# Seven products over all sixteen blocks, sums on GpSimd and four weight buffers in a decoder block's input projection

## The chip, the core and the metric

The kernel runs on one core of a Trainium2 chip. The metric is the device time of one launch in microseconds (us); the time before is 2086.86 us, the median of three runs (2086.74 to 2087.18). PE is TensorE's matmul queue and PEld its weight loads, DVE is VectorE, ACT is ScalarE, POOL is GpSimd, SP the engine that issues most transfers.

## The reference, cut to what matters

The program is one decoder block over 512 positions of width 2048 in float32: an RMSNorm, one input projection whose columns are shared out among two attention mixers (8 heads of dilated attention, 8 heads of compressed, selected and window attention), an output projection, a SwiGLU FFN of width 5632, and a final RMSNorm. What the change touches is the input projection of the normed input:

```
h = rmsnorm(x, norm1_g)        # 512 x 2048
z = h @ w_in                   # the columns are q, k, v of both mixers
```

A column block of `w_in` (128 columns) is a tensor called qb, qa, ka, va, ks, kw, vs or vw in the kernel. 2048 rows are 16 blocks of 128. The norm's per-position factor is applied behind the product (tile `r`), the gain `norm1_g` ahead of it.

## The kernel before, in words

Every float32 product is made from three matmuls (function `mm`, lines 302 to 304): both operands are split into a high part (a rounded copy, written by ACT) and a low part (source minus high, written by DVE); high times high, high times low and low times high are added up in PSUM. Weights arrive by DMA as units of 128x1024 float32 in five tiles called `raw` and are split into tiles called `w`; the unit of that work is a half, at most 128x512, called a `Job`: `first` (line 176) has ACT write the high part, `second` (line 190) has DVE write the low part and then runs `post`, which may form sums in `raw` for later halves or load the next unit. `next_half` hands PE the halves in order; when PE's code comes to half i, the code of ACT's high part for half i+3 and of DVE's low part for half i+2 has been put out. Every engine runs its own instructions strictly in that order.

Two column blocks (qb with qa, ka with va, and so on) form a pair, and a pair is computed by a scheme with seven products in place of eight (Strassen and Winograd), over two column blocks, two halves of the positions (`LO`, `HI`, 256 each) and two halves of the 2048 rows. Here a half of the rows has M = 7 blocks, so 14 of the 16 blocks are in the scheme: products P1 to P7, each 7 blocks times 3 matmuls of 256 positions. The two blocks left over are computed directly: X for the first column block, Y for the second, each 2 blocks times 3 matmuls of 512 positions. The first operands (tiles `ah`/`al` for the plain ones, T2, T3 and T4 for sums) are made once, during the first column blocks (`mix_parts`); the weights' sums are made for each pair:

- P1's operand is a unit as loaded; a transfer on POOL's queue with an accumulating write (line 137) forms the first operand of P5.
- Behind P5's second half DVE adds two units into P6's operand (line 236), and POOL issues an accumulating transfer that makes P7's operand (line 242).
- Behind P2's halves POOL issues accumulating transfers from tile to tile (line 248) that make P3's operand; for ks/vs DVE does it.

There are 17 pairs, called pair 0 to pair 16 here: ka/va of head 0, then qb/qa and ka/va of heads 1 to 7, with ks/kw and vs/vw ahead of head 4. The order within a pair is the tuple `PAIR` (line 221). Behind each half `side_hook` puts out one step of the attention of the head before (scores `psc`, transposes `pt`, products `po`, all on PE; soft maximum on DVE and ACT). `AFTER_T` is a table of halves whose split weights are placed 32 words in (`MH`) and not 16 (`WH`). Five `w` tiles take turns. Pair 0 runs while the first operands' sums for blocks 4 to 6 are still being made. After the pairs come the output projection (`pab`) and the FFN, which is 1446 us of the time.

## Time and profile before

| what | value |
|---|---|
| time, median of 3 runs | 2086.86 us |
| time of the profiled execution | 2088.05 us |
| its span (first to last instruction) | 2086.3 us |
| PE / PEld busy | 2070.6 us (99%) / 1993.7 us (96%) |
| DVE busy | 1752.7 us (84%) |
| ACT busy | 1355.5 us (65%) |
| POOL busy | 389.3 us (19%) |
| granted TensorE clock | 0.998 |
| the 17 pairs with the attention between them | 147.0 to 608.6 us |

A row of the timeline gives the start in us from the span's start, the duration in us, the engine, the line, the operation, the tiles (output<-inputs), the form and the count; in brackets stands idle time of the engine just ahead and who ended it. Matmuls are pipelined, so a matmul's own duration is longer than what it costs: the cost is the distance from one start to the next. A group row gives count, busy us, mean ns of one, idle us ahead and who ended it.

### The profile page before, as it was taken

The page shows a single profiled execution, that of the slowest core. Times are in us where ns is not written, and L with a number is a line of the kernel's source. Part 1 is how long each engine was busy: PE and PEld are TensorE (multiplying, and loading weights), DVE is VectorE, ACT ScalarE, POOL GpSimd, SP SyncE. Part 2 cuts the span into 40 slices and gives each one's busy share as a digit, 9 for nine tenths or more (in the row PEclk, how much of TensorE's full clock was granted, in tenths as well). Part 3 has the DMA queues.
Part 4 walks back from the last instruction along what each step waited for, and adds up shares of the span by engine and source line. Part 5 has one row for each costly group of instructions (what it writes and reads, how often), then busy time and mean ns, then how long its engine had stood idle before and what let it go on. Part 6 is the DMA issues. An engine that isn't in the chain of part 4 may idle for free.

```text
span 2086.3 us, 44180 instructions
## 1 busy us (share of the span) xinstructions
PE 2070.6 (99%) x16297; PEld 1993.7 (96%) x16297; DVE 1752.7 (84%) x3831; ACT 1355.5 (65%) x3355; POOL 389.3 (19%) x487
## 2 busy tenths in 40 slices
PE   9999999999999999999999999999999999999998
PEld 8789999999988889999999999999999999999997
DVE  6778888788887589989989898988889898888885
ACT  6566666566664356585767667685857676676856
POOL 0011111111120002021322213130303122030323
PEclk9999999999999999999999999999999999999999
DMA  7466665666564235366776869694847567494982
GB/s 243 156 208 163 164 154 135 168 155 146 146 217 161 97 106 175 109 215 161 185 190 168 211 146 225 152 213 118 210 130 189 147 169 175 133 211 123 217 245 94
DMA packets 138298, 351.02 MB, mean 168 GB/s; under 512 B 15328, under 2 KB 39392, under 8 KB 138080
## 3 DMA queue, kind: packets, MB, share of 16 engines
q1 hardware_dynamic: 76384, 235.44, 33.8%
q0 software_dynamic: 61552, 112.69, 29.1%
q8 instruction: 128, 2.10, 0.4%
q14 instruction: 90, 0.74, 0.1%
q10 hardware_dynamic: 144, 0.07, 0.0%
HBM read 268.89 MB, written 72.35 MB: 164 GB/s over the span
## 4 chain that ended last, share of the span: by engine, by line
PE 95%; DVE 2%; DMA 2%; ACT 1%; issue 0%; POOL 0%; SPq 0%; DVEq 0%; POOLq 0%; ACTq 0%
PE P L302 18%; PE P L304 18%; PE P L303 18%; PE pp L304 5%; PE pp L302 5%; PE pp L303 5%; PE pab L298 3%; PE pab L299 3%; PE pab L297 3%; PE pd L302 1%; PE pd L303 1%; PE pd L304 1%; PE pt L969 1%; PE pp L299 1%; PE pp L298 1%; PE pp L297 1%
## 5 line engine op out<-in xcount | busy, mean ns | idle before, releaser
L176 ACT ACTIVATE w<-raw 128x512 fp32r<-128x512 f32 (+2 forms) x1058 | 598.7, 594 | 300.5 <-DVE raw L1348 121.3
L190 DVE TENSOR_TENSOR w<-raw,w 128x512 fp32r<-128x512 f32 (+2 forms) x1024 | 659.3, 658 | 112.0 <-ACT w L176 109.7
L302 PE MATMUL P<-ah,w 128*128 128x256 f32 x1616 | 447.1, 277 | 0.0
L304 PE MATMUL P<-ah,w 128*128 128x256 f32 x1616 | 447.1, 277 | 0.0
L303 PE MATMUL P<-al,w 128*128 128x256 f32 x1616 | 446.8, 276 | 0.0
L304 PEld LDWEIGHTS P<-ah,w 128*128 128x128 f32 x1616 | 303.5, 188 | 0.3 <-DVE w L190 0.2
L302 PEld LDWEIGHTS P<-ah,w 128*128 128x128 f32 x1616 | 303.6, 188 | 0.1
L303 PEld LDWEIGHTS P<-al,w 128*128 128x128 f32 x1616 | 303.5, 188 | 0.0
L1697 POOL DMA_DIRECT2D sums<-stg x240 | 198.3, 874 | 429.1 <-ACT P L1690 150.8
L214 DVE TENSOR_TENSOR w<-raw,w 128x256 fp32r<-128x256 f32 x480 | 186.7, 420 | 28.2 <-ACT w L210 26.1
L1348 DVE TENSOR_TENSOR raw<-raw 128x512 f32<-128x512 f32 x274 | 188.5, 688 | 3.4
L210 ACT ACTIVATE w<-raw 128x256 fp32r<-128x256 f32 x480 | 177.0, 410 | 4.8 <-DVE raw L1426 4.8
L302 PE MATMUL pp<-ah,w 128*128 128x256 f32 (+1 forms) x544 | 164.1, 302 | 0.5 <-DVE pp L726 0.5
L304 PE MATMUL pp<-ah,w 128*128 128x256 f32 (+1 forms) x544 | 160.3, 295 | 1.5 <-DVE w L190 1.1
L303 PE MATMUL pp<-al,w 128*128 128x256 f32 (+1 forms) x544 | 159.2, 293 | 0.0
L1690 ACT ACTIVATE stg<-P 128x256 f32<-128x256 f32 x280 | 105.5, 381 | 15.3 <-DMA sums<-stg 5.8
L304 PEld LDWEIGHTS pp<-ah,w 128*128 128x128 f32 x544 | 102.3, 188 | 6.0 <-DVE w L190 2.9
L1352 POOL DMA_DIRECT2D raw<-in_wst_dram x40 | 34.3, 859 | 379.5 <-ACT w L176 174.9
L302 PEld LDWEIGHTS pp<-ah,w 128*128 128x128 f32 x544 | 102.7, 189 | 2.6 <-issue 0.6
L303 PEld LDWEIGHTS pp<-al,w 128*128 128x128 f32 x544 | 102.6, 189 | 1.9
L302 PE MATMUL pp<-T,w 128*128 128x256 f32 x357 | 101.7, 285 | 0.0
L297 PE MATMUL pab<-ah,w 128*128 128x512 f32 x256 | 100.6, 393 | 0.0
(399 smaller groups left out, 6161.7 us busy)
## 6 DMA issues: line engine op xcount, KB each, us to landing
raw<-in_wst_dram SPq DMA_DIRECT2D x390, 512.0 KB, 4.3
sums<-stg POOLq DMA_DIRECT2D x160, 256.0 KB, 7.0
raw<-in_wst_dram POOLq DMA_DIRECT2D x34, 448.0 KB, 6.6
raw<-in_wst_dram POOLq DMA_DIRECT2D x40, 256.0 KB, 4.7
sums<-stg POOLq DMA_DIRECT2D x80, 128.0 KB, 6.5
xc<-in_xt_dram SPq DMA_DIRECT2D x16, 256.0 KB, 3.5
bias<-in_bias_dram SPq DMA_DIRECT2D x16, 256.0 KB, 3.6
hs<-in_xt_dram SPq DMA_DIRECT2D x16, 256.0 KB, 5.2
```

The source lines that it names most:

```text
L176: act.activation(h, src, AF.Copy, scale=sign)
L190: dve.tensor_tensor(l, src, h.bitcast(F32), op=OP.subtract)
L210: act.activation(h, src(), AF.Copy)
L214: dve.tensor_tensor(l, src(), h.bitcast(F32), op=OP.subtract)
L297: pe.matmul(o, wh, mh, start=start, stop=False)
L298: pe.matmul(o, wh, ml, start=False, stop=False)
L302: pe.matmul(o, wh, mh, start=start, stop=False, skip_group_check=True)
L303: pe.matmul(o, wh, ml, start=False, stop=False, skip_group_check=True)
L304: pe.matmul(o, wl, mh, start=False, stop=stop, skip_group_check=True)
L1348: return lambda: dve.tensor_tensor(o(), o(), x(), op=OP.add)
L1690: return lambda: act.activation(o, a, AF.Copy)
L1697: return lambda s=sums[x]: pool_e.dma_start(kept_sums[k][:, q:q + n, :], s, **how)
```

## The change

M becomes 8: each of the seven products runs over 8 blocks, in two halves of 4, and X and Y are gone. A pair has 14 halves of 128x512 in place of 16 of 512, 384 or 2 times 128. P2's second half stands behind P6 now: P1 P1 P5 P5 P2 P6 P6 P2 P7 P7 P3 P3 P4 P4. The weights' sums behind P5 and P2 are made by GpSimd instructions on the tiles, not by DVE and by accumulating transfers; P7's operand is the difference of P6's and P4's. The three sums of the first operands are made by GpSimd for blocks above 4, with another sign for T2, and the order of these blocks is 4, 7, 5, 6. The eighth block's T2 and T3 lie in the fifth `w` tile (`w4`, called `tx`) and its T4 in free places of the attention's tile `et`; from the first pair to the output projection four `w` tiles take turns. The table `AFTER_T` is a new one for the new numbering (60 entries).

```diff
-M = 7
-MC = 128 * M
+M = 8
+KEPT = 7
...
+    w_used = {f"w{n}": n - 5 for n in range(5)}
+
     def wsplit(even):
-        return both(wp, 512, MH if even else WH, tag=turn("w", 5), name="w")
+        i = state["split"]
+        tag = min((t for t in w_used if t != "w4" or not n_few <= i < n_out), key=w_used.get)
+        w_used[tag] = i
+        return both(wp, 512, MH if even else WH, tag=tag, name="w")
...
-    PAIR = ("P1", "P5", "P2", "P6", "X", "P7", "P3", "Y", "P4")
+    PAIR = (("P1", 0), ("P1", 1), ("P5", 0), ("P5", 1), ("P2", 0), ("P6", 0), ("P6", 1), ("P2", 1), ("P7", 0), ("P7", 1),
+            ("P3", 0), ("P3", 1), ("P4", 0), ("P4", 1))
...
         def add(n, m, c):
-            dve.tensor_tensor(raws[u + n][:, c], raws[u + n][:, c], raws[u + m][:, c], op=OP.add)
+            pool_e.tensor_tensor(raws[u + n][:, c], raws[u + n][:, c], raws[u + m][:, c], op=OP.add)
 
         def after_p5(c):
-            if c.stop == MC:
+            add(0, 1, c)
+            if c.start:
                 for k in COLS:
-                    add(0, 1, k)
-                pool_e.dma_start(raws[u + 1][:, :MC], wst[u][:, :MC], accum_op=OP.add)
+                    pool_e.tensor_tensor(raws[u + 1][:, k], raws[u][:, k], raws[u + 3][:, k], op=OP.subtract)
 
         def after_p2(c):
-            if units[u][1] in ("ks", "vs"):
-                add(2, 0, c)
-            else:
-                pool_e.dma_start(raws[u + 2][:, c], raws[u][:, c], accum_op=OP.add)
+            add(2, 0, c)
+            if c.start:
+                load_to(u + 6)
...
         def sums():
-            dve.tensor_tensor(y[:, HI], y[:, HI], x[:, HI], op=OP.subtract)
-            dve.scalar_tensor_tensor(x[:, HI], y[:, HI], -1.0, x[:, LO], op0=OP.mult, op1=OP.subtract)
-            dve.scalar_tensor_tensor(x[:, LO], x[:, HI], -1.0, y[:, LO], op0=OP.mult, op1=OP.subtract)
+            if i > 4:
+                pool_e.tensor_tensor(y[1], y[1], x[:, HI], op=OP.subtract)
+                pool_e.tensor_tensor(x[:, HI], y[1], x[:, LO], op=OP.add)
+                pool_e.tensor_tensor(x[:, LO], x[:, HI], y[0], op=OP.subtract)
+                return
...
-        for name in PAIR:
-            if name in "XY":
-                h, l = next_half()
-                now_in[0] = 0
-                p = a if name == "X" else b
-                for k in range(2):
-                    c = slice(128 * k, 128 * k + 128)
-                    mm(p, h[:, c], l[:, c], ah[:, 2 * M + k, :], al[:, 2 * M + k, :], False, False)
...
+        for name, part in PAIR:
+            p, c = place_of[name]
+            h, l = next_half()
+            now_in[0] = 1
+            for n in range(4):
+                k = 4 * part + n
+                w = slice(128 * n, 128 * n + 128)
+                mm(p[:, c], h[:, w], l[:, w], *mix_at(operand[name], k), name == "P1" and k == 0,
+                   name in ("P3", "P4") and k == M - 1)
```

Three places show how instructions move. The first is PE in pair 0, behind P6. Before, X stands there (the first three of its six rows; tile `pp` is the pair's PSUM bank, `psc` an attention step):

```order
L299 MATMUL psc<-kall,qb 128x288
L953 MATMUL psc<-sm,tmp 128x32 [waits DMAHW3_49]
L302 MATMUL pp<-ah,w 128x512 [waits Activation_49]
L303 MATMUL pp<-al,w 128x512
L304 MATMUL pp<-ah,w 128x512 [waits DVE_49]
```

In the changed kernel P2's second half stands there, in twelve matmuls of 256 in place of X's six of 512 (the first three are shown):

```order
L285 MATMUL psc<-kall,qb 128x288
L969 MATMUL psc<-sm,tmp 128x32 [waits DMAHW3_49]
L288 MATMUL pp<-ah,w 128x256 [waits Activation_49]
L289 MATMUL pp<-al,w 128x256
L290 MATMUL pp<-ah,w 128x256 [waits DVE_49]
```

What moved is X's work, into the products; the attention's steps around it stay.

The second place is POOL's queue over one pair in the middle. Before it holds only the issues of transfers:

```order
L242 DMA raw<-in_wst_dram 128x896 [waits DMASW5_49,DMASW6_49,DMASW1_49,DMAHW0_49,DVE_49,Activation_49]
L137 DMA raw<-in_wst_dram 128x896 [waits DMAHW5_49,DMAHW3_49,DMASW2_49]
L248 DMA raw<-raw 128x512 [waits DMASW4_49,DMAHW1_49,DMASW3_49,DVE_49]
L248 DMA raw<-raw 128x384 [waits DVE_49]
L1158 DMA o_69<-oh 128x512 [waits Activation_49]
```

In the changed kernel it holds six sums, in the order P6's two halves, P7's two, P3's two:

```order
L226 TENSOR_TENSOR raw<-raw 128x512 [waits DMAHW3_49,DMASW2_49,DVE_49]
L226 TENSOR_TENSOR raw<-raw 128x512 [waits DVE_49]
L232 TENSOR_TENSOR raw<-raw 128x512 [waits DMAHW5_49,Pool_49]
L232 TENSOR_TENSOR raw<-raw 128x512 [waits Pool_49]
L137 DMA raw<-in_wst_dram 128x1024 [waits DMAHW6_49]
L226 TENSOR_TENSOR raw<-raw 128x512 [waits DMAHW4_49,DVE_49]
L226 TENSOR_TENSOR raw<-raw 128x512 [waits DVE_49]
L1174 DMA o_77<-oh 128x512 [waits Activation_49]
```

Of four transfers one is left; six instructions came in, and three of them wait only for DVE or POOL itself.

The third place is ACT in pair 0, from the high part of P5's second half on. Before, T2, T3 and T4 of a block (`T_748` and so on) wait for DVE, and P7's weights wait for a transfer:

```order
L176 ACTIVATE w<-raw 128x384 [waits DVE_49]
L562 ACTIVATE T_748<-mx 128x256 [waits DVE_49]
L562 ACTIVATE T_749<-my 128x256
L562 ACTIVATE T_750<-mx 128x256 [waits DVE_49]
L176 ACTIVATE w<-raw 128x128 x2
L176 ACTIVATE w<-raw 128x512 [waits DMASW3_49,PE_49]
L905 ACT_TABLE_LOAD
```

In the changed kernel P6's two halves and the last block's T2 and T4 wait for POOL:

```order
L177 ACTIVATE w<-raw 128x512 [waits Pool_49]
L177 ACTIVATE w<-raw 128x512 [waits PE_49,Pool_49]
L571 ACTIVATE T_748<-mx 128x256 [waits Pool_49]
L571 ACTIVATE T_749<-my 128x256
L571 ACTIVATE T_750<-mx 128x256 [waits Pool_49]
L778 ACTIVATE slots<-pp 128x256 [waits PE_49,Activation_49]
L177 ACTIVATE w<-raw 128x512
L177 ACTIVATE w<-raw 128x512 [waits DVE_49,PE_49]
L921 ACT_TABLE_LOAD
```

What moved is the waited-for engine: a sum on GpSimd stands ahead of P6's weights and of the last block's operands, and no transfer stands ahead of P7's weights.

More of the change, by code (lines that the diff above doesn't have):

```diff
@@ L136, in load_to @@
             if units[u][0] == "pair" and units[u][4] == 0:
-                later(3 if pos["half"] else 0, lambda t=t, u=u: pool_e.dma_start(t[:, :MC], wst[u + 3][:, :MC], accum_op=OP.add))
+                later(3 if pos["half"] else 0, lambda t=t, u=u: pool_e.dma_start(t, wst[u + 3], accum_op=OP.add))
             if units[u] == ("quad", 0, 1):
@@ L253, in pair_jobs @@
         js = []
-        for name in PAIR:
-            if name in "XY":
-                n = 2 * int(name == "Y")
-                js.append(Job(lambda n=n: [(raws[u + n + i][:, MC:], 1.0 - n) for i in range(2)], even=True,
-                              pieces=True, post=more(7 if n else 5)))
-                continue
-            n = {"P1": 1, "P5": 0, "P6": 0, "P2": 2, "P7": 1, "P4": 3, "P3": 2}[name]
-            for c in COLS:
-                post = {"P5": lambda c=c: after_p5(c), "P2": lambda c=c: after_p2(c)}.get(name)
-                if c.stop == MC:
-                    post = {"P7": more(6), "P4": more(8)}.get(name, post)
-                js.append(Job(part(n, c), post=post, even=len(jobs) + len(js) in AFTER_T))
+        for name, k in PAIR:
+            n = {"P1": 1, "P5": 0, "P6": 0, "P2": 2, "P7": 1, "P4": 3, "P3": 2}[name]
+            c = COLS[k]
+            post = {"P5": lambda c=c: after_p5(c), "P2": lambda c=c: after_p2(c)}.get(name)
+            if k:
+                post = {"P7": more(6), "P3": more(7), "P4": more(8)}.get(name, post)
+            js.append(Job(part(n, c), post=post, even=len(jobs) + len(js) in AFTER_T))
         return js
     for u, d in enumerate(units):
+        if d == ("in", "qb", 0, 0):
+            n_few = -(-len(jobs) // 5) * 5
         if d[0] == "pair":
@@ L428, in block_kernel, with mix_at @@
         mixed[n] = tuple(a[:, b:b + M, c] for a in (ah, al))
+    def mix_at(n, i):
+        return (beyond if n in beyond and i == KEPT else {n: [t[:, i, :] for t in mixed[n]]})[n]
+    beyond = {}
     def tmp(n, name="tmp"):
@@ L511, in block_kernel @@
     hooks = [0]
-    mix_in = {}
+    mix_in, mix_y = {}, {}
     raw = []
@@ L519, in mix_load @@
                 t = area(n)
-                mixed[n] = tuple(t[:, at:at + M * 256].rearrange("p (k c) -> p k c", c=256) for at in (0, M * 256))
-        if i == 4:
+                mixed[n] = tuple(t[:, at:at + KEPT * 256].rearrange("p (k c) -> p k c", c=256)
+                                 for at in (0, KEPT * 256))
+                beyond[n] = None
+        if i == KEPT:
+            x = ap_.tile([128, S], F32, tag="slots", name="mx")
+            y = [late["pool"].tile([128, 384], F32, tag=t, name="my")[:, :256] if t else None for t in ("e2", None)]
+        elif i == 4:
             t = late["pool"].tile([128, 2 * S + 64], F32, tag="qa", name="mxy")
@@ L535, in mix_load_y @@
     def mix_load_y(i):
-        pool_e.dma_start(mix_in[i][1], xt[M + i])
+        y = mix_in[i][1]
+        if i < KEPT:
+            pool_e.dma_start(mix_y[i], xt[M + i])
+            return
+        y[1] = late["pool"].tile([128, 384], F32, tag="e1", name="my")[:, :256]
+        for c, t in zip((LO, HI), y):
+            pool_e.dma_start(t, xt[M + i][:, c])
     def raw_load():
@@ L591, in lows @@
             low("T2", x[:, HI])
-            low("T3", y[:, HI])
+            low("T3", y[1])
             low("T4", x[:, LO])
@@ L1236, in block_kernel @@
     late["pool"] = attn.enter_context(tc.tile_pool(name="attn2", bufs=1))
-    et_h, et_l = (t.rearrange("p (a b) -> p a b", b=128) for t in both(late["pool"], 13 * 128, MH, name="et"))
+    et = placed(late["pool"], 26 * 128, MH, name="et").rearrange("p (a b) -> p a b", b=128)
+    et_h, et_l = et[:, :13, :], et[:, 13:, :]
     late["e3"] = late["pool"].tile([128, 4, 3, 32], F32, name="ecs")
@@ L1289, in block_kernel @@
             raw_load()
-            for i in range(4, M):
+            for i in (4, 5, 7, 6):
                 mix_load(i)
-            for i in range(4, M):
-                mix_load_y(i)
+                if i < KEPT:
+                    mix_load_y(i)
             SCALE_X, SCALE_Y, DIFF, SUMS, HIGHS, LOWS = range(6)
```

103 lines of the change are left out of this document (49 added, 54 removed).

## The prediction

> **What bounds the kernel now.** I read the page's shares and chain first, then the stage table, then the distance from one matmul's start to the next.
>
> ```profile
> span 2086.3 us, 44180 instructions
> PE 2070.6 (99%) x16297; PEld 1993.7 (96%) x16297; DVE 1752.7 (84%) x3831; ACT 1355.5 (65%) x3355; POOL 389.3 (19%) x487
> PE 95%; DVE 2%; DMA 2%; ACT 1%; issue 0%; POOL 0%; SPq 0%; DVEq 0%; POOLq 0%; ACTq 0%
> ```
>
> PE is busy 99% of the span and is 95% of the chain that ended last. So time is won by giving PE less to stream, and lost where PE waits. The stages that the change touches (us, then busy us and count of PE, PEld, DVE, ACT, POOL): before the pairs, pair 0, a qb/qa pair, a ka/va pair, the stretch behind the pairs.
>
> ```profile
> 110.00:147.00 37.00, 36.98 (x196) 31.18 (x194) 26.32 (x54) 24.73 (x54) 6.22 (x11) 1.00 0.72 228
> 147.00:173.20 26.20, 24.89 (x187) 23.40 (x186) 23.63 (x75) 18.41 (x54) 3.41 (x4) 1.00 0.67 173
> 229.10:258.20 29.10, 28.95 (x222) 27.80 (x221) 24.05 (x66) 17.94 (x46) 5.15 (x6) 1.00 0.60 149
> 469.30:497.60 28.30, 28.30 (x220) 27.36 (x219) 24.29 (x79) 19.41 (x58) 4.93 (x6) 1.00 0.61 152
> 608.60:640.00 31.40, 30.20 (x154) 24.79 (x153) 20.82 (x48) 17.87 (x39) 1.60 (x3) 1.00 0.42 142
> ```
>
> PE is idle for 1.31 us in pair 0 (26.20 - 24.89), 0.15 and 0.00 us in the two later pairs, and 1.20 us behind the pairs. DVE has 4 to 5 us to spare in a pair, POOL over 20. Almost nothing but PE's own stream is left to win in the pairs.
>
> **The stream.** All of the 17 pairs' matmuls of 512 positions and, as one of two groups, those of 256:
>
> ```profile
> L302 PE MATMUL pp<-ah,w 128*128 128x512 f32 x68 | 28.3, 416 | 0.0
> L302 PE MATMUL pp<-ah,w 128*128 128x256 f32 x476 | 135.8, 285 | 0.5 <-DVE pp L726 0.5
> ```
>
> X and Y are 68 x 3 = 204 matmuls of 512; they go. Seven products get one more block, 7 x 3 = 21 matmuls of 256 in each pair, 357 in all. What one costs is the distance of starts, and the trace has two levels. At the fast one, X of one pair (six matmuls, first start to the next half's start) and a run of 51 matmuls of 256:
>
> ```profile
> 273.24 0.39 PE L302 MATMUL pp<-ah,w 128*128 128x512 f32 x1
> ...
> 274.60 0.28 PE L302 MATMUL pp<-T,w 128*128 128x256 f32 x1
> ```
>
> ```profile
> 398.02 0.28 PE L302 MATMUL pp<-ah,w 128*128 128x256 f32 x1
> ...
> 403.80 0.40 PE L302 MATMUL pp<-ah,w 128*128 128x512 f32 x1
> ```
>
> That is 1.36/6 = 0.2267 us and 5.78/51 = 0.1133 us: a matmul of 512 costs exactly two of 256, so splitting it up costs nothing by itself. At the slow level, which follows transposes until a half with the other placement has passed, five of 512 and nine of 256:
>
> ```profile
> 243.87 0.39 PE L303 MATMUL pp<-al,w 128*128 128x512 f32 x1
> ...
> 245.03 0.40 PE L297 MATMUL psc<-ka,qa 128*128 128x512 f32 x1
> ```
>
> ```profile
> 266.80 0.28 PE L302 MATMUL pp<-ah,w 128*128 128x256 f32 x1
> ...
> 267.86 0.29 PE L297 MATMUL psc<-kall,qb 128*128 128x288 f32 x1
> ```
>
> 1.16/5 = 0.232 us and 1.06/9 = 0.1178 us. All fast: 204 x 0.2267 = 46.2 us go, 357 x 0.1133 = 40.4 come, -5.8. All slow: 47.3 against 42.1, -5.3. I take **-5.5**; the ends are old ones fast and new ones slow, -4.1, and the reverse, -6.9.
>
> The new placement table moves the levels of the 2499 matmuls that stay (147 x 17). X and Y always had the other placement and so ended slow stretches; without them the new order has, by my count of halves behind transposes, about five in a hundred more at the slow level: 2499 x 0.05 x 0.0045 = 0.6 us. I take **+0.4**, bounds -0.6 to +0.8.
>
> **DVE's and ACT's work.** The groups of the splits and of the sums that go:
>
> ```profile
> L190 DVE TENSOR_TENSOR w<-raw,w 128x512 fp32r<-128x512 f32 x119 | 81.5, 685 | 14.4 <-ACT w L176 14.4
> L190 DVE TENSOR_TENSOR w<-raw,w 128x384 fp32r<-128x384 f32 x118 | 65.2, 553 | 4.2 <-ACT w L176 3.6
> L190 DVE TENSOR_TENSOR w<-raw,w 128x128 fp32r<-128x128 f32 x34 | 8.3, 287 | 0.5 <-ACT w L176 0.5
> L188 DVE SCALAR_TENSOR_TENSOR w<-raw,w 128x128 fp32r<-128x128 f32 x34 | 8.3, 285 | 0.0
> L236 DVE TENSOR_TENSOR raw<-raw 128x512 f32<-128x512 f32 x19 | 13.0, 687 | 0.1
> ```
>
> For each pair DVE loses four small splits (1.14 us) and two sums (0.69 and about 0.55), and seven splits grow from 384 to 512 (7 x 0.132 = 0.92): -1.46 us.
>
> **GpSimd's sums** come in, six of 128x512 a pair. The trace has only sums of 128x256, at the end of the kernel:
>
> ```profile
> L1964 POOL TENSOR_TENSOR sacc<-sacc,sqt x24: 732/758/1112, 2033.8 to 2070.6; 128x256 f32<-128x256 f32 x24
> 2061.25 0.88 POOL L1964 TENSOR_TENSOR sacc<-sacc,sqt 128x256 f32<-128x256 f32 x1 [0.38 <-ACT sqt L1962]
> 2062.51 0.77 POOL L1964 TENSOR_TENSOR sacc<-sacc,sqt 128x256 f32<-128x256 f32 x1 [0.39 <-ACT sqt L1962]
> 2061.77 0.90 DVE L1952 TENSOR_TENSOR hs<-hs,r 128x512 f32<-128x512 f32 x1
> 2063.05 0.78 DVE L1952 TENSOR_TENSOR hs<-hs,r 128x512 f32<-128x512 f32 x1
> 2064.41 0.68 DVE L1952 TENSOR_TENSOR hs<-hs,r 128x512 f32<-128x512 f32 x1
> ```
>
> One of 512 lies between one of 256 (0.74 us) and twice the slowest ordinary one (1.76 us); I take 1.5, since work doubles and a fixed part doesn't: 9 us of POOL a pair, which has room. The last three rows show a price: DVE's sum of two SBUF tiles takes 0.68 us alone, 0.90 and 0.78 us where a GpSimd sum runs into it. So a GpSimd sum of 256 takes 0.10 to 0.22 us from DVE, one of 512 perhaps double, 0.2 to 0.44: 1.2 to 2.6 us a pair if each meets such work. Against -1.46 that is -0.3 to +1.1 us on 24.3 busy of 28.3: DVE stays short of PE. [...]
>
> The sums' lateness: P5's first low part is written about when PE starts the half two ahead, then the sum, then ACT's high part of P6, wanted three halves (4 us of matmuls) ahead of P6. There is about 1 us to spare, and the transfers that ACT waited for (the 3.19 us below) go. **The four `w` tiles** let ACT start a half only when PE has left the one four before; by the starts of ACT's rows most high parts come later than that anyway, and the others stand well ahead of PE. Both edits at **+0.5** for the 16 later pairs: bounds -0.8 (all idle there is) and +4 (0.25 us a pair).
>
> **Pair 0.** The stalls:
>
> ```profile
> 150.07 0.36 PE L302 MATMUL pp<-ah,w 128*128 128x256 f32 x1 [0.46 <-DVE pp L726]
> 153.71 0.39 PE L304 MATMUL pp<-ah,w 128*128 128x256 f32 x1 [0.69 <-DVE w L190]
> 165.16 0.38 PE L304 MATMUL pp<-ah,w 128*128 128x256 f32 x1 [0.16 <-DVE w L190]
> 159.57 0.63 ACT L176 ACTIVATE w<-raw 128x512 fp32r<-128x512 f32 x1 [3.19 <-DMA raw<-in_wst_dram]
> ```
>
> They are 1.31 us (some 1.8 by starts, since a matmul's end is modelled). DVE is late because it makes the sums for blocks 5 and 6 and P6's weights; these 6 + 2 instructions go to GpSimd, one block's splits and one difference come. What is late next is POOL: the last block's three sums stand behind P6's two sums and P7's two. P5's second low part ends near 150.3, four sums of 1.5 take POOL to 155.0, T2 of the last block is ready near 156.8 and split at 157.6; PE wants it in the third block of P6's second half, near 157.9. It just fits; at 1.76 us a sum PE waits about 1 us. I take **-1.0** for pair 0, bounds -1.8 and +1.5.
>
> **Behind the pairs** PE waits for DVE twice:
>
> ```profile
> 610.74 0.50 PE L1037 MATMUL po<-et 96*128 96x512 f32 x1 [0.39 <-DVE et L1032]
> 612.84 0.50 PE L298 MATMUL pab<-al,w 128*128 128x512 f32 x1 [0.68 <-DVE al L394]
> ```
>
> With 15 calls of the attention's step a pair in place of 17, head 7's last steps come two calls later; the compressed branch's `po` gets twelve matmuls of 512 (2.7 us) ahead of it, and the window's `po` loses two of the three groups of six that covered its transposes' split (5.2 us of cover become 2.5). **-0.3**, bounds -1.1 and +2.5.
>
> **The sum.** -5.5 + 0.4 + 0.5 - 1.0 - 0.3 = -5.9 us, made on the profiled span of 2086.3 us. That execution took 2088.05 us, 1.75 us around its span, and is 1.2 us above the median; the difference is taken off the median: 2086.86 - 5.9 = **2081.0 us**, 0.28% faster. What a measurement of this kernel can tell from no change is about 0.2%, 4.2 us.
>
> **The rivals.**
> *The gain goes back into waits* (0.21): pair 0 waits for POOL's queue behind its four sums (+1.5), the attention's end is uncovered (+2.5), the later pairs lose 0.1 us each (+1.6): with -5.1 from the stream, 2086.9 + 0.5 = 2087; half of it gives 2084. For it: pair 0's row of DVE, 23.63 of 26.20, has no room, and ACT's P6 weights now wait for POOL. Against: 3.19 us of ACT's idle time go.
> *Slower, DVE bound by GpSimd* (0.17): every GpSimd sum holds DVE up for its whole length. Six of 1.76 us, of which some 45% meet work with two SBUF inputs (14 splits of 0.685 us alone are 9.6 of DVE's 24.3), take 4.8 us a pair; DVE then has 24.3 - 1.5 + 4.8 = 27.6 us of work in a pair of 27.9, and unevenly. It decides from about 3.5 us of DVE a pair on; a wait of 0.5 to 1 us in each of 16 pairs makes +8 to +16, less 5.5: 2089 to 2097. Against: the rows above show a quarter of that price.
> *The levels don't move as counted* (0.06): all the products at the fast level, stalls gone: 2078.
>
> **How the numbers follow.** The forecast has 0.56, with a range of its own from 2078.5 to 2083. The range that is to hold 8 in 10 leaves out most of the slower rival: 2077.5 to 2088.5. Faster by over 0.2% means below 2082.7: nearly all of the forecast, the last rival and a little of the first, 0.62; within 0.2%, the first rival in the main, 0.22; slower, 0.16.
>
> **What would show it.** In the changed profile: no form of 128x512 under `pp` in the pairs and 153 more matmuls (357 - 204); starts 0.113 or 0.118 us apart; GpSimd's sums of 512 at 1.2 to 1.76 us; DVE's splits of 512 below 0.75 us in the mean (above 0.85 the slower rival holds); PE's idle time in pair 0 under 1 us, and in the later pairs under 0.2 us each; ACT's waits for POOL at P6 under 1 us. I am wrong if the pairs' stretch, 461.6 us, shrinks by less than 4 us.

## The result, and the profile after

The changed kernel takes **2118.12 us** (median of 4 runs, 2116.54 to 2120.37), against 2087.02 us (4 runs, 2086.74 to 2089.76) for the kernel before beside it: a ratio of 1.0147, 95% interval 1.0129 to 1.0164. It is slower by about 31 us where 5.9 us less was forecast, and outside the range. One of the four runs of the kernel b_pool below was slower by some 44 us at a lower granted clock (2173.51 us, 0.942) and is left out of its numbers.

The first lines of the page of the changed kernel:

```profile
span 2116.8 us, 44392 instructions
PE 2073.7 (98%) x16450; PEld 2000.7 (95%) x16450; DVE 1808.0 (85%) x3723; ACT 1363.5 (64%) x3293; POOL 506.3 (24%) x554
PE 91%; DVE 6%; ACT 2%; issue 1%; DMA 1%; SPq 0%; DVEq 0%; ACTq 0%
```

PE has 153 matmuls more, as counted, and is still busy 98% of the span; the difference is in its idle time. The table by stages of the changed kernel (us, then busy us and count of PE, PEld, DVE, ACT, POOL, then granted clock, DMA share, GB/s): all 17 pairs, pair 0, a ka/va pair, a qb/qa pair, the stretch behind the pairs.

```profile
146.84:635.55 488.71, 462.17 (x3680) 448.57 (x3679) 433.04 (x969) 299.22 (x740) 193.50 (x166) 0.99 0.45 123
146.84:180.69 33.85, 25.37 (x196) 24.73 (x195) 30.89 (x70) 18.90 (x50) 13.56 (x12) 0.90 0.37 110
488.80:517.92 29.12, 28.44 (x227) 27.73 (x226) 25.47 (x67) 19.32 (x53) 10.76 (x9) 1.00 0.44 118
239.12:268.56 29.44, 28.81 (x233) 27.98 (x232) 26.10 (x58) 18.88 (x43) 11.76 (x9) 1.00 0.43 119
635.55:667.00 31.45, 27.56 (x144) 22.96 (x145) 20.64 (x49) 15.02 (x35) 0.88 (x2) 1.00 0.30 97
```

The same stretch of the pairs in the kernel before, from its table:

```profile
147.00:608.72 461.72, 459.62 (x3532) 442.00 (x3530) 378.24 (x1076) 293.69 (x805) 81.74 (x104) 1.00 0.62 158
```

The pairs are 27.0 us longer (488.7 against 461.7). PE's idle time in them goes from 2.1 us (461.72 - 459.62) to 26.5 us, and DVE, with 107 instructions fewer, is busy 54.8 us more. Behind the pairs PE is idle for 3.9 us in place of 1.2.

What PE waited for from 140 to 700 us, in the table of waits of the changed kernel (us in all, times, longest):

```profile
PE pp L288 <- ACT pp L776: 12.7, 11, 8.3
PE pp L288 <- DVE slots L757: 5.3, 6, 2.1
PE po L1053 <- DVE et L1048: 3.6, 3, 1.3
PE pp L288 <- DVE tmp L807: 2.4, 3, 1.1
PE pt L985 <- DVE st L890: 2.4, 1, 2.4
```

Of these only the one for `po` stood in the table of the kernel before (140 to 680 us), with 0.4 us; the largest row there was for DVE's low parts:

```profile
PE pp L304 <- DVE w L190: 1.1, 3, 0.7
PE po L1037 <- DVE et L1032: 0.4, 1, 0.4
```

In the changed kernel L776 is the copy of P1's result into the first half of tile b. L757 is DVE's sum behind P6, ahead of P7. L807 reads tile a out at a pair's end. L1048 and L890 are DVE's steps of the attention.

DVE's longer time is in few groups (147 to 640 us of the changed kernel; count, busy us and mean ns of one, idle us ahead):

```profile
L180 DVE TENSOR_TENSOR w<-raw,w 128x512 fp32r<-128x512 f32 x240 | 206.3, 875 | 3.8 <-ACT w L177 3.6
L894 DVE TENSOR_SCALAR e<-e,st,gates 128x512 f32<-128x512 f32 x16 | 16.0, 1001 | 0.6
L232 POOL TENSOR_TENSOR raw<-raw 128x512 f32<-128x512 f32 x34 | 53.9, 1604 | 0.0
```

The second of these groups in the kernel before (147 to 608.7 us):

```profile
L878 DVE TENSOR_SCALAR e<-e,st,gates 128x512 f32<-128x512 f32 x16 | 8.7, 547 | 0.6
```

The splits of 512 took 0.685 us each before and take 0.875 now; the product of `e` with its factors took 0.547 us and takes 1.001. Of the splits that start in this stretch 171 meet no GpSimd sum, 0.683 us in the mean, and 68 overlap one, 1.353 us, up to 3.466. Over all of DVE's instructions the lengthening is 73 us, 4.3 us a pair. DVE's instructions that read PSUM, and all of ACT's, have the same length with and without a GpSimd sum beside them (0.691 and 0.688 us for DVE's 512-wide reading of `psc`, 0.627 us both ways for ACT's 512-wide high part).

How it comes about is seen in pair 0, in the timeline of the changed kernel (start, duration, both in us):

```profile
152.39 1.65 POOL L226 TENSOR_TENSOR raw<-raw 128x512 f32<-128x512 f32 x1 [0.63 <-DVE w L180]
152.84 1.48 DVE L576 SCALAR_TENSOR_TENSOR tx<-mx,tx 128x256 fp32r<-128x256 f32 x1
154.00 2.85 POOL L232 TENSOR_TENSOR raw<-raw 128x512 f32<-128x512 f32 x2
154.24 1.48 DVE L578 TENSOR_TENSOR tx<-my,tx 128x256 fp32r<-128x256 f32 x1
155.64 1.48 DVE L578 TENSOR_TENSOR et<-mx,et 128x256 fp32r<-128x256 f32 x1
157.22 0.38 ACT L775 ACTIVATE slots<-pp 128x256 f32<-128x256 f32 x1 [4.03 <-DVE et L578]
157.63 0.39 ACT L776 ACTIVATE pp<-slots 128x256 f32<-128x256 f32 x1
158.07 0.58 PE L288 MATMUL pp<-ah,w 128*128 128x256 f32 x1 [8.28 <-ACT pp L776]
```

A low part of 256, 0.41 us alone, takes 1.48 us three times running. The first ends at 154.32, 0.28 us behind the sum that ends at 154.04; the last at 157.12, 0.27 us behind the pair of sums that ends at 156.85. DVE waits until the GpSimd instruction is over and then does its work. All 52 splits of 512 from 147 to 640 us that start within a sum and outlast it end 0.546 to 0.575 us behind it. The reverse holds too: the 39 sums of 512 that came to a split under way took 1.52 to 1.76 us, against 1.30 us for the two that met none of these DVE instructions. By these rows the one stands until the other's whole instruction is over, and they don't share a rate: 33 of those 39 sums end 1.13 to 1.16 us behind the split they met, and in the other six the split ends 0.56 us or more behind the sum.

The last three rows show a second thing. PE's 8.28 us of idle time ends with the copy L776, that stands behind L775 on ACT, and L775 waits for the last low part of the eighth block, because `slots` is the buffer (one tile) in which that block's `x` lay. How much of the pause each of the two makes is seen in a_slots and a_dve below.

### The profile page after: what moved, and what is told of

It reads as the page before. It is cut to its first block, busy times and chain, and to the rows that moved or that the text cites. A ratio compares the mean times of both kernels' runs of the same rounds, so it can differ in the third digit from the quotient of the medians.

```text
span 2116.8 us, 44392 instructions
## 1 busy us (share of the span) xinstructions
PE 2073.7 (98%) x16450; PEld 2000.7 (95%) x16450; DVE 1808.0 (85%) x3723; ACT 1363.5 (64%) x3293; POOL 506.3 (24%) x554
## 4 chain that ended last, share of the span: by engine, by line
PE 91%; DVE 6%; ACT 2%; issue 1%; DMA 1%; SPq 0%; DVEq 0%; ACTq 0%
PE P L288 18%; PE P L290 18%; PE P L289 18%; PE pp L288 4%; PE pp L290 4%; PE pp L289 4%; PE pab L284 3%; PE pab L283 3%; PE pab L285 3%; DVE w L180 2%; PE pd L288 1%; PE pd L290 1%; PE pd L289 1%; PE pt L985 1%; DVE e L894 1%; PE pp L284 1%
## 5 line engine op out<-in xcount | busy, mean ns | idle before, releaser
L177 ACT ACTIVATE w<-raw 128x512 fp32r<-128x512 f32 x990 | 600.4, 627 | 305.8 <-DVE raw L1365 122.4
L180 DVE TENSOR_TENSOR w<-raw,w 128x512 fp32r<-128x512 f32 x990 | 713.3, 733 | 94.1 <-ACT w L177 91.7
L288 PE MATMUL pp<-ah,w 128*128 128x256 f32 x544 | 157.3, 289 | 15.2 <-ACT pp L776 12.7
L226 POOL TENSOR_TENSOR raw<-raw 128x512 f32<-128x512 f32 x68 | 100.0, 1477 | 227.0 <-DVE w L180 119.1
L290 PE MATMUL pp<-ah,w 128*128 128x256 f32 x544 | 152.5, 280 | 0.0
L289 PE MATMUL pp<-al,w 128*128 128x256 f32 x544 | 152.1, 280 | 0.0
```

The source lines that it names most:

```text
L177: act.activation(self.h, self.src(), AF.Copy)
L180: dve.tensor_tensor(self.l, self.src(), self.h.bitcast(F32), op=OP.subtract)
L226: pool_e.tensor_tensor(raws[u + n][:, c], raws[u + n][:, c], raws[u + m][:, c], op=OP.add)
L288: pe.matmul(o, wh, mh, start=start, stop=False, skip_group_check=True)
L289: pe.matmul(o, wh, ml, start=False, stop=False, skip_group_check=True)
L290: pe.matmul(o, wl, mh, start=False, stop=stop, skip_group_check=True)
```

## Where the time went, counted

To tell stream from waits I took, from 140 us to the last matmul of the output projection, the distance from each matmul's start to the next. What exceeds the usual distance of the form (0.114 us for 256 positions, 0.227 for 512) by more than 0.06 us is a wait where PE was idle in it, and "stretched" where it was not (half clock, or the matmul just behind a wait); all else is the stream. In us:

| kernel | stretch | stream | stretched | waits |
|---|---|---|---|---|
| before | 656.9 | 643.6 | 8.0 | 5.3 |
| changed | 686.7 | 638.6 | 12.4 | 35.7 |

The stream is 5.0 us shorter: 5.5 less and 0.4 more were forecast, -5.1. The stretched part grows by 4.4 and the waits by 30.4 us, and these make the result (-5.0 + 4.4 + 30.4 = 29.8 of the 30.5 us between the two spans).

## The experiments

Differences are against the kernel before beside them (the changed kernel stands at +31 us there, ratio 1.0147); the counts are made as in the table above. Four kernels undo one part of the change each.

### a_copy: the copy behind P5 again

```diff
             if name == "P1":
                 s = ap_.tile([128, 2, 256], F32, tag="slots", name="slots")
                 act.activation(s[:, 0, :], a[:, LO], AF.Copy)
-                act.activation(b[:, LO], s[:, 0, :], AF.Copy)
             elif name == "P5":
+                act.activation(b[:, LO], s[:, 0, :], AF.Copy)
```

> The changed kernel with one edit: the second copy behind P1 (P1's half of tile b written from `slots`) stands behind P5 again, as before the change. Theory 1, GpSimd's sums hold DVE up for their whole length and that is the whole loss in pairs 1 to 16: 0 to -2 us (2116 to 2118), since the copy's wait of 0.45 us in twelve pairs is filled by the next wait for DVE. Theory 2, the copy's new place is a cost of its own: the 6.5 us of PE's waits for that copy in pairs 1 to 15 go, and about 2.7 us (P5's 24 matmuls) of the 8.4 us in pair 0 are covered: -6 to -9 us (2109 to 2112).

Measured: 2113.97 us, ratio 1.0130 (1.0115 to 1.0146), +27 us: 4 us won, between the two, though the intervals of the two ratios overlap. All of the 14.9 us (by starts) that PE waited for this copy are gone, but the waits fall by 3.3 us only (35.7 to 32.4). The first rows of its table of waits:

```profile
PE pp L288 <- DVE slots L757: 6.8, 7, 2.1
PE po L1053 <- DVE et L1048: 5.6, 5, 1.7
PE pp L288 <- ACT slots L775: 3.2, 1, 3.2
```

In pair 0 PE waits 3.2 us for the copy into `slots`, one product later, and elsewhere for DVE: 6.8 us for L757 in place of 5.3, 5.6 for L1048 in place of 3.6.

### a_slots: `slots` of pair 0 in a tile of its own

```diff
-                s = ap_.tile([128, 2, 256], F32, tag="slots", name="slots")
+                if late_fill:
+                    s = late["pool"].tile([128, 2 * S + 64], F32, tag="ka", name="slots0")[:, :S]
+                    s = s.rearrange("p (h c) -> p h c", c=256)
+                else:
+                    s = ap_.tile([128, 2, 256], F32, tag="slots", name="slots")
```

> The changed kernel with one edit: in pair 0 alone `slots` is a tile of its own, in the place of ka's raw blocks, and not the one buffer in which the last block's x lies. Theory 1 (that shared buffer makes the pause of 8.4 us in pair 0 and the half clock behind it): pair 0 goes from 33.9 us to 25 to 27 us, in all -7 to -9 us (2109 to 2111). Rival (the pause is DVE's lateness behind GpSimd's sums, and the buffer only the place where it shows): PE waits for the last block's T2 or T4 in place of it; -2 to -4 us (2114 to 2116).

Measured: 2116.99 us, ratio 1.0144 (1.0129 to 1.0159), +30 us. The waits of pair 0 and its end (146 to 181 us of this kernel):

```profile
PE pp L288 <- ACT pp L780: 4.1, 1, 4.1
PE pp L290 <- DVE w L180: 1.7, 2, 0.9
```

The gain of 1 us is smaller than even the rival said, and lies within the spread of the runs. The pause is halved (8.3 to 4.1 us), so the shared buffer made half of it; PE waits for the same copy again, not for T2 or T4 as the rival had it. The rest is ACT, which comes to the copies late: it stood for 2.52 us until DVE had read out qa (L813, done at 151.30 us). DVE had worked without a pause from 146.7 us on, and two of its rows there were lengthened by GpSimd's sums, by about 0.55 us each. Two low parts are late behind the pause. Pair 0 takes 32.2 us in place of 33.9.

### a_dve: the weights' sums on DVE

```diff
         def add(n, m, c):
-            pool_e.tensor_tensor(raws[u + n][:, c], raws[u + n][:, c], raws[u + m][:, c], op=OP.add)
+            dve.tensor_tensor(raws[u + n][:, c], raws[u + n][:, c], raws[u + m][:, c], op=OP.add)
...
-                    pool_e.tensor_tensor(raws[u + 1][:, k], raws[u][:, k], raws[u + 3][:, k], op=OP.subtract)
+                    dve.tensor_tensor(raws[u + 1][:, k], raws[u][:, k], raws[u + 3][:, k], op=OP.subtract)
```

> The changed kernel with the six weights' sums of each pair on DVE in place of GpSimd, at the same places of the order. Theory 1 (a GpSimd sum holds DVE for its whole length): DVE's splits of 512 go back from 0.875 to about 0.69 us in the mean, but DVE has 6 x 0.69 = 4.1 us more work of its own in a pair, about what it lost by being held (some 70 us in 17 pairs, 4.1 a pair): the time stays within 6 us of 2118 (2112 to 2124). Rival (the sums are late because they stand in POOL's queue; DVE is not held): DVE makes each sum in half the time, no wait for POOL is left, and its splits stay as they are: -8 to -15 us (2103 to 2110).

Measured: 2120.33 us, ratio 1.0160 (1.0144 to 1.0175), +33 us. As theory 1 has it: the splits are back at 0.686 us in the mean (147 to 640 us), and nothing is won.

```profile
L180 DVE TENSOR_TENSOR w<-raw,w 128x512 fp32r<-128x512 f32 x238 | 160.9, 686 | 5.6 <-ACT w L177 5.4
```

A sum that GpSimd makes costs DVE about what DVE needs to make it (4.3 us a pair held, against 6 x 0.69 = 4.1 us of its own), so it is no relief at all. The pause of pair 0 stays too, at 9.0 us: the three low parts of the eighth block are back at 0.41 to 0.42 us each, but four sums of DVE's own now stand ahead of them. So the pause comes from a late DVE, held or with more of its own to do, together with the shared buffer.

### a_sums and a_sums2: the weights' sums as before the change

In both, P6's sums are on DVE and P7's and P3's are accumulating transfers. a_sums also puts P2's halves together again; a_sums2 leaves them around P6. The edit that both share:

```diff
-            add(0, 1, c)
             if c.start:
                 for k in COLS:
-                    pool_e.tensor_tensor(raws[u + 1][:, k], raws[u][:, k], raws[u + 3][:, k], op=OP.subtract)
+                    add(0, 1, k)
+                pool_e.dma_start(raws[u + 1], wst[u], accum_op=OP.add)
...
-            add(2, 0, c)
+            if units[u][1] in ("ks", "vs"):
+                add(2, 0, c)
+            else:
+                pool_e.dma_start(raws[u + 2][:, c], raws[u][:, c], accum_op=OP.add)
```

> The changed kernel with the weights' sums made as before the change (P6's on DVE behind P5's second half, P7's and P3's by accumulating transfers, P3's of ks and vs on DVE) and P2's second half ahead of P6 again, which these transfers need. Theory 1 (GpSimd's hold on DVE makes the waits of pairs 1 to 16): DVE's splits of 512 at 0.69 us, its busy time in a ka/va pair back to about 24 us, and PE's waits for DVE and for the copy behind P1 shrink: -12 to -18 us (2100 to 2106); pair 0's pause is shortened by about 4 us but stays. Rival (four w tiles and the copy's place make the waits): -0 to -6 us (2112 to 2118).

> The changed kernel in its own order (P2's second half behind P6), with the weights' sums as before the change: P6's two on DVE, P7's and P3's by accumulating transfers, P3's of ks and vs on DVE. Theory 1 (GpSimd's hold on DVE, some 4 us a pair, makes most of the waits in pairs 1 to 16; the 2124 us of the kernel with P2's halves together came from P7 losing its cover behind P6): -8 to -14 us against the changed kernel's 2118 (2104 to 2110), no wait for DVE's sum ahead of P7 above 0.3 us. Rival (the order makes them: the copy ahead of P5, X's and Y's place, four w tiles): -3 to +2 us (2115 to 2120).

Measured: a_sums 2123.60 us, ratio 1.0173 (1.0156 to 1.0190), +36 us, slower than the changed kernel and foreseen by neither theory; a_sums2 2110.95 us, ratio 1.0123 (1.0108 to 1.0138), +26 us, 5 us better than the changed kernel, between the two. The waits in a_sums:

```profile
PE pp L289 <- ACT pp L777: 12.8, 11, 8.3
PE pp L289 <- DVE slots L758: 8.4, 11, 1.9
```

L758 is DVE's sum behind P6. With P2's halves together nothing but a step of the attention stands between P6 and P7, so PE waits for that sum in eleven places. In a_sums2, where P2's second half stands there, only one wait of this kind above 0.15 us is left, of 0.36 us. So P2's place around P6 is worth having; what stood there before the change was X. And with the weights' sums off GpSimd the wait for the copy stays in a_sums2 (12.6 us, 8.3 of them in pair 0, as in the changed kernel): their hold wasn't its cause.

### b_pool, p_tt and p_ms: GpSimd's hold by itself

Three kernels on the side of the kernel before. b_pool gives its weights' sums to GpSimd (P7's as a difference), with M = 7, X, Y, the order and five w tiles as they were. p_tt and p_ms leave all its sums alone, take four w tiles as b_4w below does, and add, ahead of what stands behind each half of P5, three GpSimd instructions of 128x512 on a spare tile (the fifth w tile) that nobody reads: sums in p_tt, writes of a constant in p_ms. The edit of p_tt:

```diff
         def after_p5(c):
+            if not unused:
+                unused.append(wp.tile([128, 1024 + 64], F32, tag="w4", name="spare")[:, :512])
+                pool_e.memset(unused[0], 0.0)
+            for _ in range(3):
+                pool_e.tensor_tensor(unused[0], unused[0], unused[0], op=OP.add)    # p_ms: pool_e.memset(unused[0], 0.0)
```

> The kernel before with one edit: the weights' sums of each pair (P6's, P7's as a difference, P3's) are made by GpSimd instructions at their places, six a pair of 512 or 384; M = 7, X, Y, the order and five w tiles stay. Theory 1 (GpSimd's hold on DVE costs the time): DVE's splits of 512 above 0.85 us in the mean; +8 to +16 us against before (2095 to 2103). Rival (DVE's spare 4 us of a pair swallow it; the order and the four w tiles are the cost): -2 to +3 us (2085 to 2090).

> The kernel before with four w tiles in the pairs (no cost by itself: 2085.6 us) and, ahead of what stands behind each half of P5, three GpSimd sums of 512 on a spare tile that nothing else reads or writes, six a pair. It measures the hold alone, with no sum that anyone waits for. Theory (hold for the whole length): DVE's splits that meet them end 0.55 us behind GpSimd's end, the mean split of 512 above 0.85 us, +12 to +35 us (2098 to 2120). Rival (the 47 us of the kernel before with its own sums on GpSimd came from late sums): DVE's splits below 0.75 us, 0 to +4 us (2086 to 2090).

> As the kernel with six spare GpSimd sums a pair (+44 us), but with six GpSimd instructions that only write a constant to the spare tile, 512 wide. Theory (any GpSimd instruction on SBUF holds DVE for its length): DVE's splits are stretched where they meet, and the time rises with these instructions' lengths, +5 us or more. Rival (only one that reads two operands does): DVE's splits of 512 at 0.69 us throughout, -1 to +3 us (2084 to 2089).

Measured: b_pool 2129.71 us (median of three runs, 2127.26 to 2136.13), ratio 1.0218 (1.0195 to 1.0240), +45 us; p_tt 2128.85 us, ratio 1.0213 (1.0198 to 1.0228), +44 us; p_ms 2085.32 us, ratio 0.9996 (0.9986 to 1.0005), no difference. The groups of p_tt (147 to 640 us):

```profile
L249 POOL TENSOR_TENSOR spare<-spare 128x512 f32<-128x512 f32 x96 | 122.2, 1273 | 6.3
L195 DVE TENSOR_TENSOR w<-raw,w 128x512 fp32r<-128x512 f32 x117 | 89.6, 766 | 7.8 <-ACT w L181 7.6
L195 DVE TENSOR_TENSOR w<-raw,w 128x384 fp32r<-128x384 f32 x116 | 83.8, 723 | 5.1 <-ACT w L181 4.8
```

and of p_ms (the same stretch):

```profile
L249 POOL MEMSET spare<- 128x512 f32 x96 | 56.8, 592 | 4.6
L195 DVE TENSOR_TENSOR w<-raw,w 128x512 fp32r<-128x512 f32 x128 | 87.4, 684 | 13.5 <-ACT w L181 13.5
```

In p_tt no one waits for the sums, and POOL's fuller queue isn't the cause either: ACT's waits for transfers at its high parts (147 to 655 us) are 24.6 us there and 24.7 in p_ms. So the 44 us are the hold alone. Where a split of 384 met a sum it took 1.24 us, and 0.55 us elsewhere. The mean split of 512 is 0.766 us, not above 0.85 as its theory had it: only 24 of them met a sum, and 29 of the splits of 384. PE's largest wait there is for the low parts, 13.7 us in 19 places. Its some 63 us of lengthened DVE work become about 44 us of time, though DVE had 4 to 5 us to spare in each pair: of three sums one behind the other several can stop the same split (the longest took 2.34 us), and PE is only two halves behind. That this is where the prediction's slower rival was too mild is argued, not tested. Where GpSimd only writes (p_ms), 24 splits of 512 overlap it and keep their 0.683 us.

Both losses are above what the theories said (+8 to +16 and +12 to +35). b_pool loses more than the whole change, with 4.4 us of lengthened DVE work a pair against 4.3: its longest split took 3.55 us, behind several sums, and PE waited for DVE's low parts in 19 places (23.9 us). Whether the change's place for P2's second half is what spares it that was not tested.

### b_4w: four w tiles

```diff
+    w_used = {f"w{n}": n - 5 for n in range(5)}
...
     def wsplit(even):
-        return both(wp, 512, MH if even else WH, tag=turn("w", 5), name="w")
+        i = state["split"]
+        tag = min((t for t in w_used if t != "w4" or not n_few <= i < n_out), key=w_used.get)
+        w_used[tag] = i
+        return both(wp, 512, MH if even else WH, tag=tag, name="w")
```

> The kernel before with one edit: from the first pair to the output projection four w tiles take turns and not five. Theory 1 (four tiles cost nothing by themselves, since PE has left the tile of four halves ago when ACT comes to it): -1 to +2 us (2086 to 2089). Rival (ACT, held until PE has left a tile, is late with what stands behind that instruction; in the changed kernel it waited 34.5 us for PE there): +4 to +12 us (2091 to 2099).

Measured: 2085.59 us, ratio 1.0003 (0.9993 to 1.0013). Four tiles cost nothing by themselves in the kernel before. No version of the changed kernel was run with five. There ACT waits 34.5 us for PE at its high parts, but that is idle time of an engine with time to spare: in the table of PE's waits (140 to 700 us) no row is for a high part of the weights.

### b_copy and b_x: two edits of the order, in the kernel before

b_copy is the reverse of a_copy. b_x moves X ahead of P6 (the load that stood behind X, which needs P6's weights read, stands behind P6 now). The edit of b_x:

```diff
-    PAIR = ("P1", "P5", "P2", "P6", "X", "P7", "P3", "Y", "P4")
+    PAIR = ("P1", "P5", "P2", "X", "P6", "P7", "P3", "Y", "P4")
...
-                              pieces=True, post=more(7 if n else 5)))
+                              pieces=True, post=more(7) if n else None))
...
-                    post = {"P7": more(6), "P4": more(8)}.get(name, post)
+                    post = {"P6": more(5), "P7": more(6), "P4": more(8)}.get(name, post)
```

> The kernel before with one edit: the copy into b's first half stands behind P1, as in the changed kernel, and not behind P5. Theory (PE's first matmul of P5 then waits for two ACT copies of 0.39 us, whatever DVE does): +3 to +8 us (2088 to 2093). Rival (the copy's place only shows DVE's lateness in the changed kernel): -1 to +1.5 us (2084 to 2087).

> The kernel before with X moved from between P6 and P7 to between P2 and P6, the same work otherwise (the load of the next unit that stood behind X now stands behind P6). Theory (X was a cover: DVE's sum behind P6 must be done before P7's first matmul writes tile b, and X's 1.36 us hid it): a wait of 0.3 to 0.8 us ahead of P7 in each pair, +5 to +13 us (2092 to 2100). Rival (the steps of the attention behind P6 hide the sum anyway): -1 to +3 us (2085 to 2090).

Measured: b_copy 2098.43 us, ratio 1.0059 (1.0044 to 1.0074), +12 us; b_x 2100.26 us, ratio 1.0071 (1.0056 to 1.0086), +15 us. Both edits cost more than their theories said. From the table of waits of b_copy:

```profile
PE pp L302 <- ACT pp L760: 9.2, 14, 1.9
```

and of b_x:

```profile
PE pp L302 <- DVE slots L735: 4.4, 6, 2.2
PE pt L969 <- DVE st L874: 2.4, 1, 2.4
PE pab L298 <- DVE st L873: 1.9, 1, 1.9
PE pp L302 <- ACT ec L905: 1.8, 3, 0.6
```

In b_copy PE's first matmul of P5, which writes tile b as the second copy does, waits for two ACT copies (0.38 and 0.39 us, one after the other) that can't begin before P1's last matmul: by starts 12.0 us in 17 pairs, 0.7 each, with no GpSimd sum anywhere. So the wait that b_copy's theory named is there, in every pair. In b_x the sum behind P6 is uncovered, but PE waits for it in 7 of the 17 pairs and not in each (one of these waits is too short to count in the row above), and the attention's steps come at other times. By starts 12.0 of b_x's 15 us are waits and 2.6 stretched; 5.7 of the 12.0 are for the sum, as its theory has it, and most of the others are for steps of the attention. What hid these waits before were matmuls that need neither result: P5 behind the first copy and P2 behind the second, X behind the sum.

### best2, a_p0, best3 and best4: several edits together

best2 is the changed kernel with four edits: the weights' sums of a_sums2, the copy of a_copy, `slots` of a_slots, and the last three blocks' sums of the first operands on DVE. a_p0 is best2 without the first of them (the weights' sums stay on GpSimd). best3 reads tile a out right behind P3. best4 gives each pair 17 calls of the attention's step again.

```diff
 best3
-                later(0, lambda: (add(a[:, HI], a[:, HI], s[:, 0, :]), x(a)))
+                (add(a[:, HI], a[:, HI], s[:, 0, :]), x(a))
 best4
-                if n == 1 and name == "P4":
+                if n == 1 and (name == "P4" or (name, part) in (("P2", 1), ("P3", 1))):
                     side_hook[0](0.5)
...
-                side_hook[0](1)
+                side_hook[0](0.5 if name in ("P2", "P3") else 1)
```

> The changed kernel in its own order with four edits together: weights' sums as before the change (2111 us by itself), the copy of b behind P5 (-4 us by itself), pair 0's `slots` as a tile of its own (-1 us by itself), and the last three blocks' sums of the first operands on DVE. Theory (the costs are separate ones: GpSimd's hold, the copy's place, pair 0; what is left are the covers that X and Y were): pair 0 below 28 us, the time 2092 to 2100 us, still 6 to 14 us above before. Rival (with the waits gone the shorter stream shows): 2079 to 2086 us.

> The changed kernel with three of the four edits (copy behind P5, pair 0's `slots`, first operands' sums on DVE); the six weights' sums of a pair stay on GpSimd. Theory (GpSimd's hold on DVE is a cost of its own): 8 to 14 us above the kernel of four edits, 2102 to 2112 us. Rival (the hold only fills waits that are there anyway): within 3 us of it.

> The kernel of the four edits with a fifth: DVE's sum behind P3 and the reading out of tile a stand in the order right behind P3 and not behind the next half's low part. Theory (Y was the cover of that reading: PE waits 1.1 to 1.3 us for tmp at the start of four pairs): -2 to -5 us against the kernel of four edits. Rival (DVE, held at that sum until PE ends P3, is late with the low parts behind it): 0 to +6 us.

> The kernel of the four edits (2101 us) with two more calls of the attention's step in each pair, in the middle of P2's and P3's second halves, so that a pair has 17 calls as before the change and not 15. Theory (with 15 calls the steps come late and close together; PE's waits for et and st, some 8 us, are theirs): -4 to -10 us (2091 to 2097). Rival (the steps' places don't matter; what is left are the covers that X and Y were): -3 to +3 us (2098 to 2104).

Measured: best2 2101.00 us, ratio 1.0078 (1.0063 to 1.0093), +16 us; a_p0 2114.97 us, ratio 1.0147 (1.0130 to 1.0164), +31 us; best3 2102.50 us, ratio 1.0083 (1.0068 to 1.0098), +17 us; best4 2104.83 us, ratio 1.0090 (1.0073 to 1.0107), +19 us.

| kernel | stretch | stream | stretched | waits |
|---|---|---|---|---|
| a_sums2 | 683.9 | 639.6 | 13.3 | 31.0 |
| a_p0 | 685.1 | 639.7 | 13.7 | 31.7 |
| best2 | 671.8 | 638.3 | 10.3 | 23.3 |
| best3 | 672.7 | 640.4 | 12.5 | 19.8 |
| best4 | 673.4 | 639.1 | 12.3 | 22.0 |

a_p0 is no faster than the changed kernel: three of the edits together win nothing as long as GpSimd makes the weights' sums. a_sums2, the fourth alone, wins 5 us. All four win 15. The causes cover each other: PE's wait for the copy lets a late DVE catch up, and where the copy is out of the way PE waits for DVE itself (6.5 us at L757 and 5.8 at L1052, its attention step, in a_p0):

```profile
PE pp L288 <- DVE slots L757: 6.5, 6, 2.1
PE po L1057 <- DVE et L1052: 5.8, 6, 1.6
```

So the weights' sums on GpSimd cost about 14 us in the kernel that is otherwise mended (a_p0 against best2), as the theory said (8 to 14), and 5 us in the one that is not.

In best2 DVE is as it was before, in its table over all the pairs:

```profile
147.50:619.40 471.90, 456.16 (x3681) 445.67 (x3679) 383.11 (x1012) 297.88 (x740) 82.80 (x107) 1.00 0.64 163
```

383 us of DVE against 378, and PE idle for 15.7 us against 2.1. What it waits for, from the table of waits of best2:

```profile
PE po L1060 <- DVE et L1055: 2.6, 2, 1.8
PE pp L291 <- DVE tmp L814: 2.4, 3, 1.1
PE pt L992 <- DVE st L897: 2.4, 1, 2.4
PE pp L293 <- DVE w L180: 2.3, 3, 1.1
PE pt L992 <- DVE et L1007: 1.8, 2, 1.0
```

best2 is a us above the theory's range and far from the rival's; its pair 0 takes 28.5 us, where the theory had below 28. There is no single place left. best3 takes PE's wait for `tmp` at the pairs' start away and is not faster, as its rival has it; a wait behind the pairs grows from 1.6 to 4.1 us:

```profile
PE pab L287 <- DVE al L383: 4.1, 1, 4.1
```

best4 gives back the calls and is not faster either, a us above its rival's range, so the number of calls was not it. Nor is it PE waiting for the four w tiles: in best2 one wait, of 1.1 us, is for a high part of the weights. The wait for `tmp` (L814, the reading out of tile a at a pair's end) fits Y, which stood between P3 and P4 and gave DVE 1.36 us more. b_x shows that X was such a cover; that Y was one too is argued from this row alone, since no kernel with Y elsewhere was run. What makes each of the remaining 16 us is open. No version here beats the kernel before.

## Why the prediction was wrong

**The stream: right.** -5.5 + 0.4 forecast, -5.0 counted in the changed kernel, -5.3 in best2. The 153 matmuls, the two levels of distances (0.113 to 0.114 and 0.116 to 0.121 us from start to start for 256 positions in the changed kernel) and 512 at the price of two 256 (0.227 us against 2 x 0.114) all held. But a shorter stream is not shorter time where other work was timed against it.

**GpSimd's price for DVE: the step that failed first, a term of the sum put too low.** The prediction took 0.10 to 0.22 us from a sum of 256 and doubled that for 512, 1.2 to 2.6 us a pair. Its own rows said otherwise, had I compared ends and not lengths. The two GpSimd sums end at 2062.13 and 2063.28, the two DVE sums beside them at 2062.67 and 2063.83: 0.54 and 0.55 us later, the same distance as in the changed kernel. DVE had waited for the end. The price was small there only because DVE came late in the sum's time. Measured: 4.3 us a pair. The prediction named the decisive point (3.5 us) and the rival, and gave it 0.17; its 4.8 us of DVE a pair were about right, its 2089 to 2097 too mild. The observation it named for that rival, splits above 0.85 us, came true (0.875).

**GpSimd's own length: right.** 1.5 us for a sum of 512; 1.48 and 1.60 in the means, 1.30 where nothing is in the way.

**The copy: no term at all.** The diff moves the copy into b from behind P5 to behind P1. The sum has no line for it. In the kernel before it costs 12 us (b_copy): ACT can start only when PE ends P1, and PE's next product waits. It asked nowhere which engine needs what the copy writes, and what PE has to do in between.

**X and Y as covers: not seen.** They were costed as 46.2 us of stream to be removed. That X hid the sum behind P6 (moving it costs 15 us in b_x) and Y perhaps the reading out of tile a wasn't asked. P2's second half took X's place (a_sums against a_sums2: it is worth some 10 us there), none took Y's.

**Pair 0: -1.0 forecast, +7.6 measured** (26.3 to 33.9 us). The prediction watched POOL's queue and the T2 that is made last. It missed that the eighth block's `x` lies in the one `slots` buffer, which the first copy behind P1 needs, and that DVE's low parts of that block would come late; a_slots gives the buffer half of the pause, and best2, with the copy's place, the buffer and all sums as before or on DVE, has pair 0 at 28.5 us. What it expected to go, the 3.19 us wait of ACT for a transfer, did go.

**Four w tiles and the sums' lateness, +0.5:** this was the whole term for the 16 later pairs, which went from 435.4 to 454.9 us. The tiles were rightly taken as free, as far as b_4w shows. The lateness was small next to the hold: ACT waited 8.7 us in all for POOL's sums, on an engine that is busy for 299 of 489 us.

**Behind the pairs: -0.3 forecast, +3.7 measured** (1477.6 to 1481.2 us from the last pair's end), outside the bounds. PE's idle time there makes 2.7 us of it (1.2 to 3.9): it waits 2.4 us for `st` (L890) and 1.5 us for a low part of `al` (L380). The rest is no more than this stretch differs by where nothing in it was changed: from the pairs' last matmul to the end it is 1477.8 us before, 1475.3 in b_4w and 1473.9 in p_ms.

**What would show it wrong** was the right test: the pairs' stretch was to shrink by 4 us, and grew by 27.

## What to carry to other kernels

Before work is moved to GpSimd to relieve VectorE, compare where the two engines' rows end: here the splits of 512 that met a GpSimd sum ended 0.546 to 0.575 us behind it, so VectorE had waited it out, several in a row too (up to 3.466 us for a split of 0.683), and that wait is in its busy time. Look too at what VectorE's instructions read: here those with one or two wide inputs in SBUF were held (0.548 us became 1.584, 0.683 became 1.353), those with an input in PSUM were not (0.691 and 0.688 us). Before matmuls are taken out of a tight order, ask of each place what waited behind them: what is saved in the stream comes back as a wait if they were the cover of another engine's step. And where several causes overlap, undo them together as well as one by one: here the three that were undone alone won 1 to 5 us each, and all four together 15.

## What the runs showed of the hardware

The wait of PE in pair 0 cost more than itself. Behind the pause of pair 0 the granted clock was a half for about 3 us, in the table by stages of the changed kernel:

```profile
149.50:157.90 8.40, 0.30 (x3) 0.10 (x1) 8.27 (x10) 2.72 (x7) 6.70 (x6) 0.78 0.00 1
157.90:159.00 1.10, 0.93 (x4) 0.93 (x5) 1.10 (x2) 0.67 (x2) 1.02 (x2) 0.50 0.00 0
160.00:161.00 1.00, 1.00 (x6) 1.00 (x6) 1.00 (x2) 0.00 (x0) 1.00 (x1) 0.51 0.00 0
161.00:162.00 1.00, 1.00 (x10) 1.00 (x10) 1.00 (x3) 0.90 (x3) 0.41 (x1) 1.00 0.00 0
```

Six matmuls in a us, then ten. The last column but two is the granted clock. The same came behind a wait of 2.13 us at 618 us (clock 0.50 from 622 to 625 us, with starts 0.21 us apart), and not behind one of 2.35 us at 654 us (clock 1.00 from 654 to 663 us); what set these two apart is not shown. The pause of pair 0 so cost its length and an estimated 1.5 us more (half of the 3 us).

DVE's product of an SBUF tile with per-partition factors (`e` by `st` and `gates`, one wide input) was held as well: 0.548 us without a GpSimd sum beside it, 1.584 us with one (512 wide). The prediction had counted only instructions with two SBUF tiles. This kind was lengthened by instructions that only write, too: in p_ms the products of `e` that ran into a GpSimd write and were lengthened ended 0.08, 0.15 or 0.22 us behind its end (128, 256 and 384 wide), and the group of 256 took 0.468 us in the mean against 0.413 before. With these about 4 us of DVE in the whole stretch, the time didn't change.
